# A hybrid attention layer on one core: the last gate's SiLU as a quotient, the first gates' SiLU and the last query's stores moved up, one unit's maxima moved into the first attention blocks, and the late w_out splits on other engines

## The chip, the cores and the metric

The kernel runs on one core of a Trainium2 chip. Its time is the device time of one execution in microseconds; three executions of the kernel before took 723.15, 723.17 and 726.25 us, median 723.17. A core has TensorE (PE; its weight loads are listed as PEld), VectorE (DVE), ScalarE (ACT), GpSimd (POOL) and SyncE (SP, which only issues DMAs). Each engine runs its own instructions in order; between engines an instruction waits for semaphores.

## The reference, cut to what matters

One layer of a diffusion backbone: a modulated RMSNorm, one projection whose columns are queries, keys, values and gates of two groups of heads, attention for each group, a SiLU gate, one output projection.

```python
h = rmsnorm(xs, norm_gain[l]) * (1.0 + scale) + shift
q_a, k_a, v_a, g_a, q_b, k_b, v_b, g_b = project(h, w_in[l], ...)
...
o_a = global_attn_latent(q_a, k_a, v_a, cache_k_a[:, l], cache_v_a[:, l])
o_b = window_attn_latent(q_b, k_b, v_b, cache_k_b[:, l], cache_v_b[:, l], sink_b[l])
xs = xs + gate * merge_out(o_a, g_a, o_b, g_b, w_out[l])

def merge_out(o_a, g_a, o_b, g_b, w_out):
    return jnp.concatenate([o_a * jax.nn.silu(g_a), o_b * jax.nn.silu(g_b)], axis=-1) @ w_out
```

There are 1024 latent tokens and 128 context tokens (nine tiles of 128), a model width of 1024, and in each group 8 query heads of 64 over 2 key heads. All is float32; the softmax subtracts the row's maximum.

## The kernel before, in words

Every float32 product is made of two rounded parts: a matrix is split into a high part (a cast) and a low part (the rest after a subtraction), and high·high, high·low and low·high are added in PSUM. So nearly each tensor that feeds TensorE costs a cast on one engine and a subtraction on another.

The stages, in order of time:

1. **Modulation, norm and the first gates** (0 to about 72 us). Tokens are normed and transposed on TensorE into `px`; ScalarE turns `px` into `hf` (L401; three buffers with the tag `hf`), VectorE casts it (L406), GpSimd subtracts (L407). While they arrive, the gates of group A for the first 768 tokens accumulate in six PSUM banks (`big`, four of 512 tokens, and `small`, two). After the loop over `j` the gates' SiLU, `put_gates` (L289), reads each bank, and a DMA stores the result to `g_dram`. Its tiles `sg` take the buffers of the tag `hf` too. Then the products for the last 384 tokens follow (`pg`, L262), first into the bank that `big[0]` held.
2. **Queries** (to about 214 us). For each group `m` and tile `t` a projection `pq`, and behind it four steps that `later(n, ...)` puts some half blocks behind: `squares`, `scale`, `rotated`, `turned`. `turned` transposes (`ptq`, L622), casts the high part `qo0q` (L625) and stores it; `low` subtracts the low part `qo1q` on VectorE (L630), and its store follows another half block later. Both stores are DMAs on ScalarE's own queue (L635), in line with its other work. There are two buffers for `qo1q`.
3. **Keys and values** (to about 270 us). Projections `pk`, then `sqk` (L763) and the value cast `v_hi` (L752) on ScalarE, a chain of some ten VectorE instructions, a doubled copy `k2k` on ScalarE (L721), a transpose `ptk` on TensorE (L727), and the low parts `klp`, `kla`, `klb` on VectorE (L745). The first three `pk` are computed during the last queries, and their chains run after them. `v_hi` and its neighbours lie where the query stage's buffers lay, and so wait for the last query stores.
4. **Gates of group B** (`gates(W_GB, 1, ...)`, to 314.9 us): twelve pieces of 24 matmuls, each closed by a SiLU. Between the matmuls stand the items of `beside[2]`: for the units in `EARLY` (units 0 and 2) the row maxima of the global scores, `pmx` (L858), with VectorE's `mx` reductions (L859), and `finish`, which makes the negated maxima `m_nat`. A transpose `ptm` (L877) and a VectorE multiplication by `diag` (L878) turn these into the last four rows of `qb`. VectorE also splits ten of the sixteen blocks of `w_out` there (`split_wo`, L1014 a cast, L1015 the subtraction, which is on GpSimd for odd blocks).
5. **Attention** (to the end). 36 units: for a tile `t`, a key head `g` and a group `m`; units 0, 2, 4, ... are global ones with nine key blocks, units 1, 3, 5, ... windowed ones with three or four. A slot is one block. In a global slot TensorE makes the scores `st` (L1097 with `qt`, L1098 with `qb`, which holds the maxima), ScalarE the exponential `pe` (L1100) and the cast `ph` (L1104), GpSimd the low part `pl` (L1108), and three slots later TensorE the values `pv` (L1118 to L1121). Between these stand items for later units: the maxima of the unit two further on at `MX_AT`, and the windowed scores `sn` (L915, L916) of the next unit at `NAT_AT`, with VectorE's mask and row minimum (L919) and ScalarE's `pen` (L905). `pmx`, `ptm`, `sn` share the two PSUM banks with the tag A; `st` has the two of tag B. The last five blocks of `w_out` are loaded and split here, at the slots of `WO_LATE`.

The order on an engine is that of the Python emission; `in_order` fixes it. `later(n, f)` runs `f` after `n` ticks, and a tick is half a projection block in stages 1 to 4 and one slot in stage 5. The exponential's table is loaded on ScalarE by an instruction of its own (L1046) behind the last SiLU.

Of the kernel before, what the change touches and what calls it, by code (L numbers as in the profile page):

```python
# [9 lines left out]
F32 = mybir.dt.float32  # L10
# [3 lines left out]
ALU = mybir.AluOpType  # L14
# [4 lines left out]
P = 128  # L19
# [16 lines left out]
PL_DVE = (4,)  # L36
LAG = 3
LEAD = 4
EARLY = (0, 2)
LOADED = 4  # L40


NAT_AT = (0, 1, 2, 3)
NAT_FIRST = (0, 1, 2, 3)
MX_AT = (-4, -3, -2, -2, -1, 4, 5, 5, 7, 7, 8, 8)
MX_FIRST = (0, 1, 2, 2, 3, 4, 4, 5, 6, 6, 7, 8)
PH_DVE = 0
MX_END = 10
SPLIT_LAG = 2
# [23 lines left out]
ROWS_AT = (1, 1, 4, 6)  # L73
KV_ORDER = [0] + list(range(1, NT))
GATE_AT = (3, 7)
QUERY_LAST = (0, 1, 2, 4)
CACHE_AT = 8
VC_AT = 6
ONES_AT = 14
# [28 lines left out]
def hybrid_step(ctx, tc, x_prompt, x_sample, cache_k_a, cache_v_a, cache_k_b, cache_v_b,  # L108
# [17 lines left out]
    def later(n, f):  # L126

        agenda.setdefault(now[0] + n, []).append(f)
# [156 lines left out]
    def put_gates(pg, m, ch, ts):  # L285

        n = ts.stop - ts.start
        sg = sg_tile[-1](f"sg{m}_{ch}_{ts.start}")[:, 0:n]
        nc.scalar.activation(sg, pg, AF.Silu)  # L289
        r0 = 512 * m + P * ch  # L290
        (nc.scalar, nc.sync)[m].dma_start(g_dram[r0 : r0 + P, ts], sg)

    def put_pair(pg, ch):

        sg = sg_tile[-1](f"sgp{ch}")
        nc.scalar.activation(sg, pg, AF.Silu)
        nc.scalar.dma_start(g_dram[P * ch : P * ch + 2 * P, 512:768].rearrange("(c p) n -> p c n", p=P),
                            sg.rearrange("p (c n) -> p c n", c=2))

    def gates(w, m, nxt, thirds):  # L300

        pieces = [(ch, slice(a, b)) for a, b in thirds for ch in range(4)]
        for ch, ts in pieces:
            pg = bank_mm(f"pg{m}_{ch}_{ts.start}")[:, 0 : ts.stop - ts.start]
            block(pg, lambda k: gate_products(pg, w, ch, ts, k), nxt, nxt and (ch, ts) == pieces[-1])
            later(1, lambda pg=pg, ch=ch, ts=ts: put_gates(pg, m, ch, ts))
            yield


# [1 line left out]
    with tc.tile_pool(name="st", bufs=2, side="right") as st:  # L311
# [129 lines left out]
        for j in range(KT + 2):  # L441
# [30 lines left out]
                first_gates(1, j - 1, 1)  # L472
            if j == 1:
                transposed(0, 5, 2, 0)
            if big_on:
                first_gates(2, j - 1)
            if j < KT:
# [24 lines left out]
        assert not second  # L502


        sg_tile.append(lambda n: st.tile([P, 512], F32, tag="hf", name=n, bufs=3))
        put_gates(big[0], 0, 0, slice(0, 512))
        for ch in range(1, 4):
            later(ch, lambda ch=ch: put_gates(big[ch], 0, ch, slice(0, 512)))
        for i in range(2):
            later(4 + i, lambda i=i: put_pair(small[i], 2 * i))  # L510
        for _ in gates(W_GA, 0, W_QA, THIRDS[2:]):
            pass
        tick()
# [37 lines left out]
    with tc.tile_pool(name="qt", bufs=2, side="right") as qt:  # L551
# [34 lines left out]
        def query(pq, m, t, tabs, n=1):  # L586

            nm = f"q{m}_{t}"
            pqv = pq.rearrange("p (h d) -> p h d", d=HD)
            v = {}  # L590

            def squares():
                sq = qt.tile([P, 8, HD], F32, tag="sq", name=f"sq{nm}")
# [25 lines left out]
            def turned():  # L619
                ptq = bank_tr(f"pt{nm}")  # L620
                for h in range(4):
                    nc.tensor.transpose(ptq[:, P * h : P * h + P], v["qf"][:, h].rearrange("p g d -> p (g d)"),  # L622
                                        ident_r.bitcast(F32))
                qo = [qt.tile([P, 512], F32R, tag=f"qo{i}", name=f"qo{i}{nm}") for i in range(2)]
                nc.scalar.copy(qo[0], ptq)  # L625
                put(qo[0], 0)
                later(1, lambda: low(ptq, qo))

            def low(ptq, qo):
                nc.vector.tensor_tensor(qo[1], ptq, qo[0], op=ALU.subtract)  # L630
                later(1, lambda: put(qo[1], 1))

            def put(part, i):
                for g in range(2):
# [372 lines left out]
            wo_big[a] = h_slot(a // 2, 2, 4 * (a % 2), f"wo_big{a}")  # L1007
        return wo_big[a][:, 512 * o : 512 * o + 512]

    def split_wo(i):  # L1010
        raw = wo_raw.pop(i)
        hi, lo = (wo_place(j, i) for j in range(2))
        wo_parts[i] = hi, lo
        nc.vector.tensor_copy(hi, raw)  # L1014
        (nc.gpsimd if i % 2 else nc.vector).tensor_tensor(lo, raw, hi, op=ALU.subtract)  # L1015


    mask = qp.tile([P, 512], BF16, name="mask", bufs=1)
# [15 lines left out]
        load_wo(i)  # L1034
    for i, at, *then in WO_STEPS:
        later(at, lambda i=i, then=then: wo_step(i, *then))
    for n, _ in enumerate(gb):
        if n == 4:
            for i in (7, 8, 9):
                load_wo(i)  # L1040
    for f in beside[2]:
        f()
    tick()
    p1.close()

    nc.scalar.add_instruction(mybir.InstLoadActFuncSet(  # L1046
        name=nc.get_next_instruction_name(), engine=mybir.EngineType.Activation, act_func_set_id=6))

    qp2.append(ctx.enter_context(tc.tile_pool(name="qp2", bufs=1, side="right")))
    w3 = ctx.enter_context(tc.tile_pool(name="w3", bufs=4, side="right"))  # L1050
# [188 lines left out]
    for s in range(len(slots) + LAG + PROMPT_END[3]):  # L1239
        tick()  # L1240
        if s < len(slots):
            live.append((slots[s], slots[s] and scores(slots[s][0], slots[s][1], slots[s][3])))
        for n, at in WO_LATE.items():
            if s == at:
                load_wo(n, w2)
                later(3, lambda n=n: split_wo(n))
        for f in due.get(s, ()):
            f()
        rate = OUTRATE if s < len(slots) and slots[s] else PADRATE
        credit = min(credit + rate, 6.0) if outq else 0.0  # L1250
        while outq and credit >= 1.0:
            outq.pop(0)()
            credit -= 1.0
        if s >= LAG and live:
            slot, parts = live.pop(0)
            if slot:
                values(*slot, *parts)
# [65 lines left out]
```

## Time and profile before

| what | value |
|---|---|
| three executions | 723.15, 723.17, 726.25 us |
| span of the profiled execution, first to last instruction | 721.3 us |
| mean granted TensorE clock | 0.993 |
| instructions | 10622 |
| DMA over the span | 78.56 MB, 109 GB/s |

The profile gives a span, and no device time of its own for that execution. The median of the three executions is 1.9 us above the span. Idle time in the profile's rows stands in square brackets, with the instruction that ended it. In the views of waits the columns are: who waited, for whom, us in total, times, longest.

### The profile page before, as it was taken

Reading aid. Unit: us, or ns where it says so; the run is one execution under the profiler, and the core shown is the slowest. Engines: PE = TensorE matmul, PEld = TensorE weight load, DVE = VectorE, ACT = ScalarE, POOL = GpSimd, SP = SyncE. Lnnn points to the kernel's source line nnn. Section 1 sums busy time; section 2 is a strip of 40 time slices with the busy share of each in tenths; the row PEclk is TensorE's granted clock in tenths of the full one; section 3 lists DMA queues with packets and bytes.
Section 4 is the critical chain, followed back from the end, with each engine's and each line's share of the span. In section 5 each row is a group of like instructions: output and inputs, shape, how many; then the busy total and the mean of one; then the engine's idle time right before and its main releaser. Section 6 shows DMA issues by size and latency. Waiting matters only on the chain. (4 is left out here: it accounts for less than half of the span.)

```text
span 721.3 us, 10622 instructions
## 1 busy us (share of the span) xinstructions
PE 698.3 (97%) x3524; PEld 559.7 (78%) x3524; DVE 457.6 (63%) x1007; ACT 411.7 (57%) x829; POOL 335.3 (46%) x355
## 2 busy tenths in 40 slices
PE   5999999999999999999999999999999999999997
PEld 2678988877777788977788888888888888887865
DVE  3466147875675872745866677577666775775653
ACT  5355411411232451158778877877787778877770
POOL 3456013332322340236666555655575557555751
PEclk9999999999999999999999999999999999999999
DMA  8961373348435115440321222121212221212323
GB/s 344 346 219 59 121 278 86 79 94 276 121 85 142 45 60 171 139 143 23 103 67 45 73 67 88 44 81 52 87 54 59 66 87 45 81 53 87 103 65 119
DMA packets 53159, 78.56 MB, mean 109 GB/s; under 512 B 6569, under 2 KB 25449, under 8 KB 52081
## 3 DMA queue, kind: packets, MB, share of 16 engines
q1 hardware_dynamic: 44928, 65.96, 28.1%
q10 hardware_dynamic: 8176, 11.94, 6.3%
q8 instruction: 28, 0.46, 0.3%
q14 instruction: 27, 0.21, 0.1%
HBM read 58.69 MB, written 19.18 MB: 108 GB/s over the span
## 5 line engine op out<-in xcount | busy, mean ns | idle before, releaser
L1108 POOL TENSOR_TENSOR pl<-pe,ph 128x512 fp32r<-128x512 f32 x130 | 167.6, 1292 | 144.7 <-DVE nm L919 67.5
L859 DVE TENSOR_REDUCE mx<-pmx 128x1 f32<-128x384 f32 x192 | 101.4, 552 | 59.5 <-PE pmx L858 58.1
L1100 ACT ACTIVATE pe<-st 128x512 f32<-128x512 f32 x146 | 86.8, 594 | 28.0 <-PE st L1098 27.1
L1104 ACT CAST ph<-pe 128x512 fp32r<-128x512 f32 x146 | 90.6, 621 | 4.8
L1118 PE MATMUL pv<-ph,v_hi 128*128 128x512 f32 x208 | 83.2, 400 | 2.2 <-DVE spare L1142 2.2
L1121 PE MATMUL pv<-pl,v_hi 128*128 128x512 f32 x208 | 82.6, 397 | 0.0
L173 POOL TENSOR_TENSOR rs_q<-ms_q,mhalf 128x8 f32<-128x8 f32 x18 | 34.8, 1931 | 82.1 <-DVE ms_q L171 82.1
L1189 PE MATMUL po<-wo,ogh 128*128 128x512 f32 x216 | 72.5, 394 | 0.2 <-DVE yt L1196 0.2
L919 DVE CUSTOM_DVE_ANT_0 sn<-sn,mask,nsink 128x512 f32<-128x512 f32 (+1 forms) x64 | 46.3, 724 | 38.3 <-PE sn L916 36.5
L858 PE MATMUL pmx<-kha,qt 128*128 128x384 f32 x192 | 61.0, 363 | 0.4 <-ACT pen L905 0.2
L1097 PE MATMUL st<-qt,kha 128*128 128x512 f32 x144 | 58.3, 405 | 1.5 <-ACT pe L1100 0.8
L1098 PE MATMUL st<-qb,kla 68*128 68x512 f32 x144 | 57.6, 400 | 1.1 <-DVE qb L878 1.1
L1120 PE MATMUL pv<-ph,v_lo 128*64 128x512 f32 x146 | 57.9, 396 | 0.0
L1121 PEld LDWEIGHTS pv<-pl,v_hi 128*128 128x128 f32 x208 | 39.4, 189 | 16.7 <-issue 0.2
L905 ACT ACTIVATE pen<-sn,nm 128x512 f32<-128x512 f32 (+2 forms) x72 | 45.0, 626 | 6.5 <-DVE nm L919 3.1
L1093 ACT CAST ph<-st 128x512 fp32r<-128x512 f32 x62 | 36.4, 587 | 19.9 <-PE st L1092 18.7
L1118 PEld LDWEIGHTS pv<-ph,v_hi 128*128 128x128 f32 x208 | 39.4, 189 | 10.5 <-ACT ogh L1154 2.4
L1189 PEld LDWEIGHTS po<-wo,ogh 128*128 128x128 f32 x216 | 40.0, 188 | 6.8 <-DVE yt L1196 0.6
L1094 DVE TENSOR_TENSOR pl<-st,ph 128x512 fp32r<-128x512 f32 x62 | 42.5, 686 | 2.3 <-ACT ph L1093 1.5
L1189 PE MATMUL po<-wo,ogl 128*128 128x512 f32 x108 | 42.6, 394 | 0.0
L594 ACT ACTIVATE sqq<-pq 128x512 f32<-128x512 f32 x18 | 10.8, 599 | 53.3 <-DMA qd<-qo0q 14.4
L858 PEld LDWEIGHTS pmx<-kha,qt 128*128 128x128 f32 x192 | 35.5, 190 | 6.2 <-DVE mx L859 1.4
(216 smaller groups left out, 1700.2 us busy)
## 6 DMA issues: line engine op xcount, KB each, us to landing
qt<-qd SPq DMA_DIRECT2D x36, 256.0 KB, 3.1
wm<-in_w_mod_ss_dram SPq DMA_DIRECT2D x8, 1024.0 KB, 5.1
qd<-qo0q ACTq DMA_DIRECT2D x36, 128.0 KB, 2.4
qd<-qo1q ACTq DMA_DIRECT2D x36, 128.0 KB, 2.4
sgl<-gd SPq DMA_DIRECT2D x36, 128.0 KB, 2.1
out_dram<-yt SPq DMA_DIRECT2D x17, 256.0 KB, 2.1
xn<-in_x_sample_dram SPq DMA_DIRECT2D x8, 512.0 KB, 7.0
wg<-in_w_mod_g_dram SPq DMA_DIRECT2D x4, 1024.0 KB, 7.9
```

The lines of the kernel that those rows point to most:

```text
L858: nc.tensor.matmul(pm[:, 0:384], lhs, kha[:, g, 3 * b : 3 * b + 3, :], start=True, stop=True)
L859: nc.vector.tensor_reduce(mx[:, h, b : b + 1], pm[:, 0:384], axis=AX.X, op=ALU.max)
L919: nc.vector.tensor_tensor_reduce(s, s, mask[:, m0 : m0 + n], -1.0, nsink[:, 4 * g + h : 4 * g + h + 1], op0=ALU.add, op1=ALU.min, accum_ou ...
L1097: nc.tensor.matmul(s, kh, qtile[i], start=True, stop=False)
L1098: nc.tensor.matmul(s, kl, qbtile[i], start=False, stop=True)
L1100: nc.scalar.activation(pe, s, AF.Exp)
L1104: nc.scalar.copy(ph, pe)
L1108: nc.gpsimd.tensor_tensor(pl, pe, ph, op=ALU.subtract)
L1118: nc.tensor.matmul(pv, two, ph, start=(b == 0), stop=False)
L1120: nc.tensor.matmul(pv[0:64, :], vl, ph, start=False, stop=False)
L1121: nc.tensor.matmul(pv, two, pl, start=False, stop=last)
L1189: nc.tensor.matmul(po[n], a, wo_parts[KT * n + k][lo], start=(k == KS[0] and p == 0), stop=(k == KS[-1] and p == 2))
```

## The change

- `EARLY` keeps unit 0 only. Unit 2's twelve `pmx` matmuls and `mx` reductions leave the gates' stage and stand in unit 0's slots 0 to 8 (`MX_FIRST`), with `finish` in slot 10 and `ptm` in slot 12. The four windowed score items of unit 1 move from slots 0 to 3 to slots 3 to 6 (`NAT_FIRST`). Unit 0's own maxima are spread over the same eight pieces as both were before.
- The last gate piece is not a SiLU on ScalarE any more but x / (1 + exp(-x)): an `Exp` on ScalarE, then an addition, a reciprocal and a multiplication on VectorE, each 128x384. The exponential's table is loaded half a piece earlier, ahead of that `Exp`.
- The first two `big` banks get their SiLU and store inside the loop at `j == KT`, ahead of the last seven `hf`.
- The last query (group B, tile 0) is turned half a block earlier, and its subtraction and both stores follow at once instead of by `later`.
- The late blocks of `w_out` are cast on ScalarE and subtracted on GpSimd, not on VectorE.

```diff
-EARLY = (0, 2)
+EARLY = (0,)
-NAT_FIRST = (0, 1, 2, 3)
+NAT_FIRST = (3, 4, 5, 6)
-MX_FIRST = (0, 1, 2, 2, 3, 4, 4, 5, 6, 6, 7, 8)
+MX_FIRST = (0, 0, 1, 1, 2, 2, 3, 4, 5, 6, 7, 8)
-QUERY_LAST = (0, 1, 2, 4)
+QUERY_LAST = (0, 1, 2, 3)
...
+    def put_quotient(pg, m, ch, ts):
+
+        n = ts.stop - ts.start
+        e = sg_tile[-1](f"e{m}_{ch}")[:, 0:n]
+        sg = sg_tile[-1](f"sg{m}_{ch}_{ts.start}")[:, 0:n]
+        nc.scalar.activation(e, pg, AF.Exp, scale=-1.0)
+        nc.vector.tensor_scalar(e, e, 1.0, None, op0=ALU.add)
+        nc.vector.reciprocal(e, e)
+        nc.vector.tensor_tensor(sg, pg, e, op=ALU.mult)
+        r0 = 512 * m + P * ch
+        nc.sync.dma_start(g_dram[r0 : r0 + P, ts], sg)
...
-            later(1, lambda pg=pg, ch=ch, ts=ts: put_gates(pg, m, ch, ts))
+            put = put_quotient if m == 1 and (ch, ts) == pieces[-1] else put_gates
+            later(1, lambda pg=pg, ch=ch, ts=ts, put=put: put(pg, m, ch, ts))
...
+            if j == KT:
+                sg_tile.append(lambda n: st.tile([P, 512], F32, tag="hf", name=n, bufs=3))
+                for ch in range(2):
+                    put_gates(big[ch], 0, ch, slice(0, 512))
...
-        sg_tile.append(lambda n: st.tile([P, 512], F32, tag="hf", name=n, bufs=3))
-        put_gates(big[0], 0, 0, slice(0, 512))
-        for ch in range(1, 4):
-            later(ch, lambda ch=ch: put_gates(big[ch], 0, ch, slice(0, 512)))
+        for ch in range(2, 4):
+            later(ch - 1, lambda ch=ch: put_gates(big[ch], 0, ch, slice(0, 512)))
         for i in range(2):
-            later(4 + i, lambda i=i: put_pair(small[i], 2 * i))
+            later(3 + i, lambda i=i: put_pair(small[i], 2 * i))
...
+            after = (lambda f: f()) if (m, t) == (1, 0) else (lambda f: later(1, f))
...
-                later(1, lambda: low(ptq, qo))
+                after(lambda: low(ptq, qo))
...
-                later(1, lambda: put(qo[1], 1))
+                after(lambda: put(qo[1], 1))
...
-    def split_wo(i):
+    def split_wo(i, late=False):
...
-        nc.vector.tensor_copy(hi, raw)
-        (nc.gpsimd if i % 2 else nc.vector).tensor_tensor(lo, raw, hi, op=ALU.subtract)
+        (nc.scalar.copy if late else nc.vector.tensor_copy)(hi, raw)
+        (nc.gpsimd if i % 2 or late else nc.vector).tensor_tensor(lo, raw, hi, op=ALU.subtract)
...
+    def load_exp():
+        nc.scalar.add_instruction(mybir.InstLoadActFuncSet(
+            name=nc.get_next_instruction_name(), engine=mybir.EngineType.Activation, act_func_set_id=6))
+
     for n, _ in enumerate(gb):
...
+        if n == 6:
+            later(2, load_exp)
...
-                later(3, lambda n=n: split_wo(n))
+                later(3, lambda n=n: split_wo(n, True))
```

How the change moves instructions, at three places. First ScalarE at the end of the queries of group B, before (`_7`, `_8`, `_0` are the tiles, `qo0q` high parts, `qo1q` low parts, `qd` the stores' target):

```order
L635 DMA qd_1_70<-qo1q_6_2172 64x512 x2
L625 CAST qo0q_8_2268<-ptq_8_2263 128x512
L635 DMA qd_1_74<-qo0q_8_2268 64x512 x2
L625 CAST qo0q_0_2278<-ptq_0_2273 128x512
L635 DMA qd_1_58<-qo0q_0_2278 64x512 x2
L635 DMA qd_1_72<-qo1q_7_2229 64x512 x2
L635 DMA qd_1_74<-qo1q_8_2269 64x512 x2
L635 DMA qd_1_58<-qo1q_0_2279 64x512 x2
L763 ACTIVATE sqk_2334<-pk_2165 128x256
```

and the same place now:

```order
L651 DMA qd_1_70<-qo1q_6_2172 64x512 x2
L641 CAST qo0q_0_2254<-ptq_0_2249 128x512
L651 DMA qd_1_58<-qo0q_0_2254 64x512 x2
L651 DMA qd_1_58<-qo1q_0_2255 64x512 x2
L641 CAST qo0q_8_2281<-ptq_8_2276 128x512
L651 DMA qd_1_74<-qo0q_8_2281 64x512 x2
L651 DMA qd_1_72<-qo1q_7_2229 64x512 x2
L651 DMA qd_1_74<-qo1q_8_2282 64x512 x2
L779 ACTIVATE sqk_2334<-pk_2165 128x256
```

Tile 0's cast and all its stores have gone ahead of tile 8's; the last store in the queue is now that of tile 8's low part, and with two buffers that part takes the buffer of tile 0's, not of tile 7's.

Second VectorE at the end of the gates of group B, as it is now (`e1_3` and `sg1_3_768` belong to the last gate piece, `qb0` to unit 0, `mx2` and `pmx2` to unit 2):

```order
L885 TENSOR_REDUCE m40_3314<-mx0_3017 128x4
L888 TENSOR_SCALAR m_nat0_108<-m40_3314 128x4
L299 TENSOR_SCALAR e1_3_3323<-e1_3_3323 128x384
L300 RECIPROCAL e1_3_3323<-e1_3_3323 128x384
L301 TENSOR_TENSOR sg1_3_768_3324<-pg1_3_768_3282,e1_3_3323 128x384
L894 TENSOR_TENSOR qb0_3312<-ptm0_3353,diag_110 4x512
L875 TENSOR_REDUCE mx2_3365<-pmx2_0_0_3366 128x1
L875 TENSOR_REDUCE mx2_3365<-pmx2_0_1_3369 128x1
```

Before, unit 0's `qb` had been made some pieces earlier, and unit 2's stood at this place with nothing of the gates ahead of it:

```order
L1015 TENSOR_TENSOR wo1_10_3344<-wraw10_3259,wo0_10_3343 128x512
L859 TENSOR_REDUCE mx2_3192<-pmx2_3_2_3350 128x1
L869 TENSOR_REDUCE m42_3361<-mx2_3192 128x4
L872 TENSOR_SCALAR m_nat1_109<-m42_3361 128x4
L878 TENSOR_TENSOR qb2_3359<-ptm2_3394,diag_110 4x512
L919 ISA sn1_0_3411,nm1_3407<-sn1_0_3411,mask_2978,nsink_105 128x384
```

Third TensorE in the first slots of unit 0, as it is now (before, each pair of `st` was followed by a pair of `sn`):

```order
L893 MATMUL ptm0_3353<-ident_r_99,m_nat0_108 4x128
L1116 MATMUL st0_0_3356<-qt0_2981,kha_2319 128x512
L1117 MATMUL st0_0_3356<-qb0_3312,kla_2320 128x512
L874 MATMUL pmx2_0_0_3366<-kha_2319,qt2_2985 128x384
L874 MATMUL pmx2_0_1_3369<-kha_2319,qt2_2985 128x384
L1116 MATMUL st0_1_3372<-qt0_2981,kha_2319 128x512
L1117 MATMUL st0_1_3372<-qb0_3312,kla_2320 128x512
L874 MATMUL pmx2_0_2_3381<-kha_2319,qt2_2985 128x384
L874 MATMUL pmx2_1_0_3384<-kha_2319,qt2_2985 128x384
```

The second matmul of the first scores reads `qb0`, whose last writer on VectorE stands behind the three instructions of the quotient.

More of the change, by code (lines that the diff above doesn't have):

```diff
@@ L1044, in hybrid_step @@
     p1.close()
-    nc.scalar.add_instruction(mybir.InstLoadActFuncSet(
-        name=nc.get_next_instruction_name(), engine=mybir.EngineType.Activation, act_func_set_id=6))
     qp2.append(ctx.enter_context(tc.tile_pool(name="qp2", bufs=1, side="right")))
```

## The prediction

> **What bounds the kernel now.** I read the page first, then the view of waits for TensorE alone, then the timeline around each of its waits. The first table of the page (engine, busy us, share of the span, instructions) says which engine to follow:
>
> ```profile
> PE 698.3 (97%) x3524; PEld 559.7 (78%) x3524; DVE 457.6 (63%) x1007; ACT 411.7 (57%) x829; POOL 335.3 (46%) x355
> ```
>
> TensorE is busy for 97%, so an edit pays only if it removes matmuls or one of the few holes between them. The holes behind the start-up are these, of which the change aims at five:
>
> ```profile
> PE ptk L727 <- DVE klp L745: 1.4, 1, 1.4
> PE ptk L727 <- ACT k2k L721: 1.2, 1, 1.2
> ...
> PE pg L262 <- ACT sg L289: 0.9, 1, 0.9
> PE st L1097 <- ACT pe L1100: 0.8, 1, 0.8
> ...
> PE st L1097 <- DVE pl L1094: 0.7, 1, 0.7
> PE sn L915 <- ACT pen L905: 0.5, 1, 0.5
> ```
>
> They sum to 5.5 us, 0.8% of the span. To these belongs a hole that no wait shows: a slower clock behind the last gate. In the windows below the columns are busy time of PE, PEld, DVE, ACT, POOL with instruction counts, then the granted clock:
>
> ```profile
> 319.00:320.00 1.00, 1.00 (x4) 0.40 (x2) 0.55 (x2) 0.97 (x3) 0.62 (x2) 0.66 0.86 265
> 320.00:321.00 1.00, 0.90 (x3) 0.61 (x3) 0.14 (x2) 0.97 (x4) 1.00 (x1) 0.50 0.96 289
> 322.00:323.00 1.00, 1.00 (x4) 0.81 (x3) 0.24 (x2) 0.97 (x3) 0.83 (x1) 0.64 0.78 266
> ```
>
> After 0.8 and 0.5 us of idling within three, the clock was halved for some 3 us, which costs up to 1.6 us more. So everything that this change can win lies near 7 us, and what it can lose is new holes of the same kind.
>
> **First gates' SiLU.** ScalarE and TensorE before:
>
> ```profile
> 68.50 2.37 ACT L401 ACTIVATE hf<-px,b_col,a_mod 128x128 f32<-128x128 f32 x5 [2.70 <-PE px L397]
> 71.89 0.60 ACT L289 ACTIVATE sg<-pg_f 128x512 f32<-128x512 f32 x1
> 72.53 0.44 PE L262 MATMUL pg<-h,whiga 128*128 128x384 f32 x1 [0.94 <-ACT sg L289]
> ```
>
> Two SiLUs of 0.60 us and two store issues (0.55 at most, half of the query's pair below) make at most 2.3 us, and ScalarE idles 2.70 us ahead of 68.50: they fit, and the wait of 0.94 goes. But the SiLU's tiles are two of the three `hf` buffers, and a store lands some 2 us after its issue (2.4 for the query's below), so the second `hf` waits for the first store and the next ones follow GpSimd with two buffers. I count the last `hf` and the last `px` transposes 0.6 us late (two transposes wait for a bank, 0.2 to 0.3 each). Net −0.35 us. Bounds: −0.94 with no delay, +0.5 if the stores land slowly. If the idle 2.70 were not there, the two SiLUs would cost their 2.3 us in front of the `hf`.
>
> **Last query's stores.** The rows around them, and the page's row of the low parts' stores with the median us from issue to landing:
>
> ```profile
> 210.70 0.39 PE L250 MATMUL pk<-whikv,h 128*128 128x512 f32 x1
> 211.35 0.68 DVE L614 TENSOR_TENSOR qfq<-qnq,gain 128x512 f32<-128x512 f32 x1
> 213.65 1.04 PE L622 MATMUL ptq<-ident_r,qfq 128*128 128x128 f32 x8
> 216.79 1.10 ACTq L635 DMA_DIRECT2D qd<-qo0q  x2
> 221.22 0.69 DVE L630 TENSOR_TENSOR qo1q<-ptq,qo0q 128x512 fp32r<-128x512 f32 x1 [5.62 <-DMA qd<-qo1q]
> 223.09 0.39 ACT L763 ACTIVATE sqk<-pk 128x256 f32<-128x256 f32 x1 [6.32 <-DMA ksin<-in_k_sin_dram]
> 225.19 0.37 ACT L752 CAST v_hi<-pk 128x256 fp32r<-128x256 f32 x1 [1.72 <-DMA qd<-qo1q]
> 229.47 0.66 PE L727 MATMUL ptk<-ident_r,k2k 128*128 128x128 f32 x4 [1.17 <-ACT k2k L721]
> 237.53 0.63 PE L727 MATMUL ptk<-ident_r,k2k 128*128 128x128 f32 x4 [1.44 <-DVE klp L745]
> ```
>
> ```profile
> qd<-qo1q ACTq DMA_DIRECT2D x36, 128.0 KB, 2.4
> ```
>
> The last subtraction (221.22) waits for a landing that frees its buffer, the stores queue behind it on ScalarE, `sqk` starts when the queue is empty, `v_hi` when the stores have landed, and the chain of keys from there is late twice on TensorE. Now tile 0's transposes stand half a block earlier, where TensorE arrives at 210.93; its operand is ready at 211.35 + 0.68 = 212.03. That is a new hole of about 1.2 us, and `ptq_8` behind it finds its bank free to within 0.1: the next projection starts 1.3 us late. ScalarE then casts tile 0 at 212.9 to 213.5, issues four stores (1.1 per pair) until 215.7, casts tile 8 at 216.0, and issues three pairs until 219.9; tile 8's low part needs tile 0's buffer, whose stores land at about 217.5, in time. So `sqk` starts at 220.0, 3.1 us sooner than 223.09. TensorE comes 1.3 us later to both `ptk`, the chain 3.1 us sooner: both holes (1.17 and 1.44) close. Net 1.3 − 2.6 = −1.3 us. Bounds: −2.6 if the operand were in time, +0.5 if the chain is not sooner at all (the old holes then swallow the new one).
>
> **End of the gates, unit 0.** The rows:
>
> ```profile
> 299.96 0.34 PE L858 MATMUL pmx<-kha,qt 128*128 128x384 f32 x1
> 300.14 0.33 PE L262 MATMUL pg<-h,whigb 128*128 128x384 f32 x1
> ...
> 315.10 0.40 PE L1098 MATMUL st<-qb,kla 68*128 68x512 f32 x1
> ...
> 324.94 0.39 PE L1097 MATMUL st<-qt,kha 128*128 128x512 f32 x1
> ...
> 326.09 0.40 PE L1097 MATMUL st<-qt,kha 128*128 128x512 f32 x1
> ...
> 328.61 0.60 PE L1092 MATMUL st<-ident_r,pen 128*128 128x128 f32 x4
> ```
>
> ```profile
> 315.01 0.49 ACT L289 ACTIVATE sg<-pg 128x384 f32<-128x384 f32 x1 [4.21 <-PE ptm L877]
> 315.52 1.28 ACT L1046 ACT_TABLE_LOAD   x1
> 316.81 0.60 ACT L1100 ACTIVATE pe<-st 128x512 f32<-128x512 f32 x1
> ```
>
> A `pmx` takes 0.18 us of TensorE, a 512 wide matmul 0.23 (five in 1.15). (1) Twelve `pmx` and one `ptm` leave the gates' stage, where TensorE has no wait: −2.2 us. (2) The table load leaves the path: `pe` could start 1.3 us sooner. (3) It can't, since the first score's second matmul needs `qb0`, which VectorE makes behind the quotient. VectorE's prices, from groups by form and a single line's view:
>
> ```profile
> L859 DVE TENSOR_REDUCE mx<-pmx 128x1 f32<-128x384 f32 x192 | 101.4, 552 | 59.5 <-PE pmx L858 58.1
> L878 DVE TENSOR_TENSOR qb<-ptm,diag 4x512 fp32r<-4x512 f32 x18 | 12.3, 682 | 7.9 <-PE ptm L877 7.8
> L954 DVE RECIPROCAL inv<-sum 128x4 f32<-128x4 f32 x18 | 3.0, 168 | 1.1 <-POOL sum L951 1.1
> L171 DVE TENSOR_SCALAR ms_k<-ssk 128x4 f32<-128x4 f32 x9 | 1.5, 170 | 0.3
> L376 DVE TENSOR_SCALAR xn<-xn,rsx x9: 753/753/1791, 10.1 to 51.7; 128x1024 f32<-128x1024 f32 x9
> ```
>
> `Exp` ends at 315.50 as the SiLU did. The addition is 0.38 (753 ns for 1024 columns, less a fixed 0.15, by 384/1024), the multiplication 0.55 like `mx`, `qb` 0.68. A reciprocal of 384 columns isn't in the trace; one of 4 columns takes 168 ns, an ordinary instruction of 4 columns 170, so no extra per element shows, and I take 0.56. With hand-overs `qb0` is ready at 317.8 instead of TensorE's 315.10: +2.75 us, all of it idle TensorE.
>
> (4) From there to unit 1's first transposes the trace took 328.61 − 315.10 = 13.5 us. Now TensorE has to do 0.23, eight pairs of `st` (3.7), thirteen `pmx` (2.3), four pairs of `sn` (1.4) and six triples of values (4.2): 11.8 us. ScalarE's load in between is what it was (nine `pe` and `ph`, four `pen`). To the 11.8 come waits of `pmx` and `sn` for the two banks, each held for 0.34 + 0.55 us with two per slot at first: between 0 and 1.9 us, I take 1.2. And the clock: 2.6 us of idling in one piece is more than the 1.3 that halved it before, so I take it as halved again for 3.2 us, 1.6 us of which some lies beside those waits: 1.3. Sum 14.3, that is +0.8. The stage: −2.2 + 2.75 + 0.8 = +1.35 us; bounds −1.0 (no bank waits, full clock) and +2.5.
>
> The Trainium skill's page "TensorE: Matmul & The Clock Gate", section "Part 1: The HAM clock gate", has the clock fall only after at least one idle window of about 3.4 us. By that the 2.6 us here would leave it at full speed and the stage would cost 0.05 instead of 1.35. The rows above do not agree: 1.3 us of idling in pieces was enough.
>
> **Late w_out.** Three casts of blocks 11, 14, 15 and two of 12, 13 move to ScalarE, two of the subtractions with them to GpSimd. The one that mattered:
>
> ```profile
> 332.24 0.69 DVE L1015 TENSOR_TENSOR wo_big<-wraw,wo_big 128x512 fp32r<-128x512 f32 x1
> 333.68 0.47 PE L1097 MATMUL st<-qt,kha 128*128 128x512 f32 x1 [0.67 <-DVE pl L1094]
> 354.52 0.51 PE L1098 MATMUL st<-qb,kla 68*128 68x512 f32 x1 [0.63 <-DVE qb L878]
> ```
>
> The subtraction delayed `pl` and TensorE waited 0.67 us at unit 2's start. That goes, but unit 2's maxima now end where unit 4's did, so its `qb` is late as theirs was, 0.63 us: zero. ScalarE's added casts (about 0.6 each, a 128x512 pass like the SiLU's) lie in its idle time beside the windowed slots; without that cover the pace of the first exponentials behind them would carry them, at most 1.2 us per unit.
>
> **Sum.** −0.35 − 1.3 + 1.35 + 0 = −0.3 us on a span of 721.3. What lies outside the span (1.9 us to the median) is not touched, so 723.17 becomes 722.9.
>
> **Rivals.** *The reciprocal works several steps per element* (slower than before): eight would add 384 x 7 x 1.04 ns = 2.8 us to `qb0`'s wait (1.04 ns per column from 552 ns for 384, less 0.15), giving 725.7; slower than before from about two steps (0.4 us) on. For it: the trace has no long one. Against it: at 4 columns it would already show 29 ns. The skill's page "VectorE: DVE Perf Modes", section "First, the fixed hardware budget", says that the reciprocal's divide runs with a repeat count of 8, which read as eight steps an element gives that time; the 168 ns speak against it.
>
> *The clock stays full*: −1.3, so 721.6. For it: the idling is in one piece and might fall across two measuring windows. Against it: the rows above.
>
> *The key chain is not freed*, because `v_hi` waits for the landing of all stores and the last one is still late: then −1.3 becomes 0, and the time 724.2. Against it: the order has four stores fewer behind the last landing.
>
> **Chances.** The forecast 0.45, the reciprocal 0.15, the full clock 0.2, the chain 0.12, mixtures 0.08. 0.5% (3.6 us, about what a measurement of this kernel can tell from no change) lies at 719.6 and 726.8. Below that only the full clock with all lower bounds comes: 0.06. Above it the reciprocal with a second slow clock or the chain's failure: 0.07. Within: 0.87. The range 720.4 to 726.0 holds the three rivals and leaves out the ends of the bounds.
>
> **What would show it.** In the profile after: the wait on `sg` at 72.5 gone; a new wait of about 1.2 us of `ptq` for `qfq`, and both waits of `ptk` gone; a wait of about 2.6 us of the first `st` (on `qb`) behind the gates; windows at half clock behind it; the reciprocal's own row near 0.56 us. It is wrong if the first `st` waits under 1.5 us, if `sqk` starts no sooner, or if a stage beyond unit 4 changes its pace.

## The result: 726.0 us, 2.85 us slower, and the profile after

The changed kernel takes 725.99 us (median of 18 runs, 724.38 to 727.07), the kernel before 723.14 us in the same session (18 runs, 721.69 to 726.25). The ratio is 1.0036, 95% interval 1.0028 to 1.0045. The forecast was 722.9 us, a gain of 0.3 us; a loss of 2.85 us came. 725.99 lies just inside the range that the prediction gave (720.4 to 726.0), but the forecast had the sign wrong. The profiled execution has a span of 724.6 us (721.3 before).

The first table of the page after says the same of TensorE as before: busy for 97%, it is what bounds.

```profile
PE 699.3 (97%) x3524; PEld 560.4 (77%) x3524; DVE 455.9 (63%) x1003; ACT 414.9 (57%) x834; POOL 338.2 (47%) x357
```

The view of waits for TensorE (who waited, for whom, us in total, times, longest) has changed in the rows that the prediction spoke of. Both `ptk` rows and the row on `sg` are gone, and a new one leads:

```profile
PE st L1117 <- DVE qb L894: 6.1, 4, 4.6
...
PE ptq L638 <- DVE qfq L630: 1.1, 1, 1.1
...
PE px L410 <- ACT hf L414: 0.5, 1, 0.5
```

One wait of 4.6 us stands where about 2.6 were forecast. VectorE's timeline at that place (start, duration, instruction, idle time before it) shows what it waits for:

```profile
312.00 0.36 DVE L299 TENSOR_SCALAR e<-e 128x384 f32<-128x384 f32 x1 [2.25 <-ACT e L298]
312.40 2.55 DVE L300 RECIPROCAL e<-e 128x384 f32<-128x384 f32 x1
314.99 0.56 DVE L301 TENSOR_TENSOR sg<-pg,e 128x384 f32<-128x384 f32 x1
315.58 0.68 DVE L894 TENSOR_TENSOR qb<-ptm,diag 4x512 fp32r<-4x512 f32 x1
```

The reciprocal takes 2.55 us; the prediction had 0.56. The addition (0.36 for 0.38), the multiplication (0.56 for 0.55) and `qb` (0.68) are as forecast. On TensorE:

```profile
311.23 0.23 PE L893 MATMUL ptm<-ident_r,m_nat 128*4 128x128 f32 x1
311.29 0.45 PE L1116 MATMUL st<-qt,kha 128*128 128x512 f32 x1
316.31 0.80 PE L1117 MATMUL st<-qb,kla 68*128 68x512 f32 x1 [4.57 <-DVE qb L894]
```

And the windows behind it (columns as in the prediction):

```profile
315.00:316.00 1.00, 0.00 (x0) 0.00 (x0) 0.97 (x2) 0.00 (x0) 0.00 (x0) 0.54 0.00 0
316.00:321.00 5.00, 4.69 (x13) 3.71 (x13) 2.85 (x7) 3.27 (x6) 2.31 (x2) 0.50 0.76 216
321.00:322.00 1.00, 1.00 (x5) 0.90 (x4) 0.48 (x2) 0.69 (x2) 0.79 (x2) 0.55 1.02 360
```

TensorE is busy again from 316.31 on (4.69 of the five us from 316), but at half the clock until about 321.9, for twice as long as in the profile before.

Where the time went is read best from five marks in TensorE's timeline: the first matmul of the first gates' last piece (`pg` at 72.53 before), the last `ptm` ahead of unit 0, the first `st<-qb` of unit 0, the first transposes of unit 1 and those of unit 3. Units are counted from 0, as in the code; in some expectations below "unit 3's maxima" are what the code calls unit 2's. The table has the time from each mark to the next, in us, one profiled execution of each kernel; the labels are those of the experiments.

| kernel | `pg` at | to `ptm` | to `st<-qb` | to unit 1 | to unit 3 | to the end of TensorE |
|---|---|---|---|---|---|---|
| before | 72.53 | 242.23 | 0.34 | 13.51 | 19.90 | 368.06 |
| after | 72.96 | 238.27 | 5.08 | 15.01 | 20.06 | 368.15 |
| u_silu | 72.46 | 238.52 | 1.00 | 13.88 | 20.07 | 367.71 |
| silu_wo | 71.43 | 238.31 | 1.00 | 13.89 | 21.27 | 367.67 |
| silu_max | 71.89 | 240.46 | 0.34 | 13.05 | 20.33 | 368.06 |
| swap | 72.92 | 238.64 | 1.00 | 18.14 | 20.07 | 367.84 |
| short_recip | 71.66 | 238.45 | 3.28 | 14.31 | 20.07 | 367.78 |
| u_max | 71.37 | 240.57 | 0.34 | 16.32 | 20.10 | 368.05 |
| lnexp | 73.20 | 239.65 | 1.00 | 13.97 | 20.07 | 368.17 |
| only_max | 72.32 | 239.85 | 1.00 | 13.91 | 21.97 | 367.77 |
| only_query | 72.51 | 240.68 | 0.33 | 13.05 | 20.23 | 368.21 |

Of the kernel after, 3.96 us are won ahead of `ptm`, 4.74 are lost from there to `st<-qb`, 1.50 from there to unit 1, 0.25 behind, and 0.43 at the start. The last is within what executions differ by anyway: the mark lies between 71.4 and 73.2 in these kernels, which hardly differ before it. The way to `ptm` differs by 1 us between executions too: a second profile of u_silu's kernel (u_silu_2) has 239.54 there, and 1.00, 13.90, 20.08 and 367.62 behind, so the gains ahead of `ptm` named below are those of single executions.

### The profile page after: what moved, and what is told of

It reads as the page before. It is cut to its first block, busy times and chain, and to the rows that moved or that the text cites. A ratio compares the mean times of both kernels' runs of the same rounds, so it can differ in the third digit from the quotient of the medians.

```text
span 724.6 us, 10639 instructions
## 1 busy us (share of the span) xinstructions
PE 699.3 (97%) x3524; PEld 560.4 (77%) x3524; DVE 455.9 (63%) x1003; ACT 414.9 (57%) x834; POOL 338.2 (47%) x357
```

## The experiments

Two theories stood at first. **A**: the whole loss is the reciprocal, which stands on VectorE ahead of unit 0's `qb`; what else was changed gains. **B**: unit 2's maxima in the first slots cost, and the reciprocal only fills a hole that would be there without it. Each kernel was timed beside the kernel before on the same chip; ratios, with their 95% intervals, are to that one (723.2 to 723.4 us); they differ by up to 0.1% from the quotients of the two medians.

**u_silu: the quotient alone undone.**

```diff
-            put = put_quotient if m == 1 and (ch, ts) == pieces[-1] else put_gates
+            put = put_gates
...
-        if n == 6:
-            later(2, load_exp)
...
     p1.close()
+    load_exp()
```

> The changed kernel with the quotient alone undone: the last gate's SiLU is one ScalarE instruction again and the Exp table is loaded after it. Everything else of the change stays, unit 3's maxima in the first blocks too. Theory A (the 2.55 us reciprocal stands on VectorE ahead of unit 0's qb, opens the 4.57 us wait on TensorE and with it the 6.5 us of half clock, and that is the whole loss): st<-qb starts about 0.4 us after ptm as before, half clock about 3 us, 719.6 to 721.6 us. Theory B (unit 3's maxima in the first blocks are what costs, by their matmuls and bank waits at half clock, and the reciprocal only fills a hole that would be there anyway): 724 us or more.

720.62 us (ratio 0.9951, 0.9931 to 0.9970). Theory A's range held, B's did not. Two of A's signs came out otherwise: `st<-qb` starts 1.00 us behind `ptm`, not 0.4, and the clock does not fall at all. A second set of runs gave nearly the same:

> The same kernel as u_silu again (the quotient undone, all else of the change kept), since that had six runs only. If its 720.6 us was the kernel and not the chip or the hour: 720.0 to 721.3 us, 2 to 3 us below the kernel before.

720.36 us (0.9966, 0.9956 to 0.9976). So by the medians the quotient costs 5.4 to 5.6 us against the SiLU and table load that it replaced, and the other four parts are worth 2.8 us together. In the table, between after and u_silu, 4.08 us of the quotient's cost lie ahead of `st<-qb` and 1.13 between there and unit 1. ScalarE with the SiLU back, from its timeline:

```profile
311.23 0.49 ACT L289 ACTIVATE sg<-pg 128x384 f32<-128x384 f32 x1 [3.85 <-PE ptm L893]
311.74 1.28 ACT L1054 ACT_TABLE_LOAD   x1
313.03 0.60 ACT L1118 ACTIVATE pe<-st 128x512 f32<-128x512 f32 x1
```

The first `pe` starts at 313.03, 2.05 us behind `ptm`; with the quotient it starts at 317.14, 5.91 us behind:

```profile
317.14 0.60 ACT L1119 ACTIVATE pe<-st 128x512 f32<-128x512 f32 x1 [5.17 <-PE st L1117]
```

The table load that the quotient was to hide takes 1.28 us; the reciprocal alone takes 2.55. In the windows the clock stays full:

```profile
311.00:314.00 3.00, 2.47 (x10) 1.42 (x9) 1.93 (x4) 2.71 (x4) 0.00 (x0) 1.00 0.30 106
314.00:317.00 3.00, 2.99 (x14) 2.05 (x14) 2.67 (x7) 2.94 (x6) 2.59 (x3) 1.00 0.92 232
317.00:320.00 3.00, 2.57 (x13) 1.79 (x11) 1.95 (x5) 2.94 (x8) 2.45 (x2) 1.00 0.84 285
```

**short_recip: the reciprocal over 96 of 384 columns.**

```diff
-        nc.vector.reciprocal(e, e)
+        nc.vector.reciprocal(e[:, 0:96], e[:, 0:96])
```

> The changed kernel with the reciprocal over the first 96 of the 384 columns; the other columns of the last gate are multiplied by 1 + exp(-x) and are not the reference's. Only the length of the reciprocal differs. Theory A: it takes 0.7 to 0.8 us if its price goes by columns; the wait at st<-qb falls by 1.8 us to 2.8 us, the half clock gets shorter too, 723.0 to 724.3 us. Theory B: 725.5 us or more. If the wait falls but the time does not, the wait was not on the path.

723.84 us (0.9995, 0.9984 to 1.0006), 2.1 us below the kernel after, inside A's range and outside B's. VectorE's and TensorE's rows of this kernel's timeline:

```profile
311.28 0.75 DVE L300 RECIPROCAL e<-e 128x96 f32<-128x96 f32 x1
...
313.39 0.54 PE L1117 MATMUL st<-qb,kla 68*128 68x512 f32 x1 [2.77 <-DVE qb L894]
```

1.80 us less of reciprocal is 1.80 us less of waiting (4.57 to 2.77), and 0.70 us less from there to unit 1 (15.01 to 14.31 in the table); the half clock lasts 3.4 us here, not 6.8.

**swap: `qb` ahead of the quotient's vector part.** The three instructions of VectorE are put off until behind `qb`; the order of the other instructions around them, on VectorE, ScalarE and TensorE, stays as it was.

```diff
         nc.scalar.activation(e, pg, AF.Exp, scale=-1.0)
-        nc.vector.tensor_scalar(e, e, 1.0, None, op0=ALU.add)
...
+        def rest():
+            nc.vector.tensor_scalar(e, e, 1.0, None, op0=ALU.add)
...
+        later(2, rest)
...
-    tick()
+    for _ in range(3):
+        tick()
     p1.close()
```

> The changed kernel with unit 0's qb ahead of the quotient's three VectorE instructions; same instructions on every engine. The reciprocal now stands ahead of unit 3's first maxima in place of qb. Theory A: the 4.57 us wait at st<-qb falls below 0.8 us; the third pmx matmul of unit 3 waits some 2 us for a bank in its place; 722.5 to 724.5 us. Theory B (the position ahead of qb does not matter, VectorE is simply short by 3.5 us in the first blocks): 725.5 to 726.5 us.

724.88 us (1.0013, 0.9998 to 1.0027): 1.1 us below the kernel after, and between the ranges of A (up to 724.5) and B (from 725.5). The wait moved, to the third `pmx`, whose bank VectorE had not read:

```profile
312.56 0.50 PE L1122 MATMUL st<-qb,kla 68*128 68x512 f32 x1 [0.49 <-DVE qb L898]
316.60 1.15 PE L878 MATMUL pmx<-kha,qt 128*128 128x384 f32 x2 [2.72 <-DVE mx L879]
```

The clock fell again, and for as long (windows of the same kernel):

```profile
315.00:316.00 1.00, 0.00 (x0) 0.00 (x0) 0.96 (x3) 0.49 (x1) 1.00 (x2) 0.86 0.00 0
...
322.00:323.00 1.00, 1.00 (x5) 0.76 (x5) 0.00 (x0) 0.17 (x2) 0.80 (x1) 0.73 1.08 319
```

In the table 4.08 us are won at `st<-qb` and 3.13 lost from there to unit 1, so the place ahead of `qb` is not the main point.

**u_max: the maxima back in the gates' stage, the quotient kept.**

```diff
-EARLY = (0,)
+EARLY = (0, 2)
-NAT_FIRST = (3, 4, 5, 6)
+NAT_FIRST = (0, 1, 2, 3)
-MX_FIRST = (0, 0, 1, 1, 2, 2, 3, 4, 5, 6, 7, 8)
+MX_FIRST = (0, 1, 2, 2, 3, 4, 4, 5, 6, 6, 7, 8)
```

> The changed kernel with the maxima alone put back into the gates' stage; the quotient stays. Unit 0's qb is then made pieces earlier and unit 2's stands behind the quotient. Theory A (the reciprocal costs by standing ahead of the first score's qb): no wait of st<-qb at the first blocks, unit 1's sn matmuls wait 0 to 1.5 us for a bank instead, clock full or half for a short time, 721.0 to 723.0 us. Rival (3.5 us of VectorE there cost wherever they stand): 724.5 us or more.

725.15 us (1.0029, 1.0016 to 1.0042), in the rival's range and only 0.8 us below the kernel after. Unit 0's `qb` is there in time, and now unit 1's `sn` waits:

```profile
317.02 0.69 PE L931 MATMUL sn<-khb,qt 128*128 128x384 f32 x1 [3.52 <-DVE qb L894]
```

Against the same kernel with the SiLU (silu_max, below) the quotient costs 1.9 us in the medians and 3.1 in the profiled executions (645.38 and 642.24, sums of the table's rows); that is less than the 5.5 us it costs with the maxima in the first slots, but a loss still. Theory A was too narrow. What counts is that VectorE is shut for 3.5 us, from the addition's start to the multiplication's end, at a moment when TensorE needs it within a slot for something: for `qb`, for a maximum's bank, or for `sn`'s.

**lnexp: the quotient without VectorE's reciprocal.** ScalarE makes 1 / (1 + exp(-x)) as exp(-ln(1 + exp(-x))); VectorE only multiplies, behind `qb`.

```diff
         nc.scalar.activation(e, pg, AF.Exp, scale=-1.0)
-        nc.vector.tensor_scalar(e, e, 1.0, None, op0=ALU.add)
-        nc.vector.reciprocal(e, e)
+        nc.scalar.activation(e, e, AF.Ln, bias=1.0)
+        nc.scalar.activation(e, e, AF.Exp, scale=-1.0)
```

> The changed kernel with unit 0's qb ahead and the quotient made by ScalarE: after exp(-x) a Ln of that plus 1 and an Exp of its negative, VectorE only multiplies. All three are of the table that the attention needs, so no load stands between. Theory A (what counts is that neither VectorE nor ScalarE holds back the first score for long): pe comes about 1.8 us behind ptm, as with the SiLU and its table load, 719.6 to 721.4 us. Rival (two more ScalarE passes ahead of the first pe open the hole again): 722 us or more.

722.50 us (0.9981, 0.9966 to 0.9997). The median lies in the rival's range (722 or more) and outside A's 719.6 to 721.4. Yet the hole that the rival named is not in the profile: `pe` starts at 314.61, 1.76 us behind `ptm`, and the table has 1.00, 13.97 and 20.07 for it where u_silu has 1.00, 13.88 and 20.07. In its profiled execution most of the difference lies ahead of `ptm`, a part of it in the last query: a subtraction waited 1.68 us for a store's landing, where u_silu's waited 0.30 (VectorE's rows of lnexp, then of u_silu):

```profile
216.44 0.69 DVE L650 TENSOR_TENSOR qo1q<-ptq,qo0q 128x512 fp32r<-128x512 f32 x1 [1.68 <-DMA qd<-qo1q]
```

```profile
214.16 0.69 DVE L646 TENSOR_TENSOR qo1q<-ptq,qo0q 128x512 fp32r<-128x512 f32 x1 [0.30 <-DMA qd<-qo1q]
```

Both kernels have the same instructions at that place, in the same order, and u_silu's own kernel waited 1.71 us there in its second profile (u_silu_2), an execution that took 720.43 us. So this wait comes in some executions and not in others, and it does not explain the median. What makes lnexp's median 1.9 to 2.1 us longer than u_silu's stays open.

**only_max: the kernel before with the maxima alone moved** (the same three lines as in u_max, the other way round).

> The kernel before with unit 3's maxima alone moved from the gates' stage to the first blocks. Theory A: ptm comes about 2.2 us sooner and the first blocks give back 0 to 2 us of it: 721.0 to 723.2 us. Theory B: 724 us or more.

723.66 us (0.9999, 0.9987 to 1.0012), above A's range and under B's 724: nothing won or lost. The table says why. 2.38 us are won ahead of `ptm` and 1.06 given back up to unit 1, as A had it; but from unit 1 to unit 3 another 2.07 go (21.97 for 19.90). VectorE's timeline there:

```profile
330.21 0.41 DVE L1014 CAST wo_big<-wraw 128x512 fp32r<-128x512 f32 x1
330.66 0.69 DVE L1015 TENSOR_TENSOR wo_big<-wraw,wo_big 128x512 fp32r<-128x512 f32 x1
331.27 0.68 DVE L1094 TENSOR_TENSOR pl<-st,ph 128x512 fp32r<-128x512 f32 x1
331.87 0.55 DVE L859 TENSOR_REDUCE mx<-pmx 128x1 f32<-128x384 f32 x1
332.34 0.17 DVE L954 RECIPROCAL inv<-sum 128x4 f32<-128x4 f32 x1
332.42 0.40 DVE L1014 CAST wo_big<-wraw 128x512 fp32r<-128x512 f32 x1
332.85 0.68 DVE L878 TENSOR_TENSOR qb<-ptm,diag 4x512 fp32r<-4x512 f32 x1
```

Three passes of late `w_out`, 1.5 us, stand on VectorE ahead of unit 2's `qb`, which is made here now, and TensorE waits 0.70 us for `pl` and 1.01 us for `qb`:

```profile
332.11 0.47 PE L1097 MATMUL st<-qt,kha 128*128 128x512 f32 x1 [0.70 <-DVE pl L1094]
...
333.59 0.50 PE L1098 MATMUL st<-qb,kla 68*128 68x512 f32 x1 [1.01 <-DVE qb L878]
```

Behind these waits the clock is halved, from 334.5 to 337.9. That is the case that the last part of the change is for.

**silu_wo: u_silu with the late w_out splits back on VectorE.**

```diff
-        (nc.scalar.copy if late else nc.vector.tensor_copy)(hi, raw)
-        (nc.gpsimd if i % 2 or late else nc.vector).tensor_tensor(lo, raw, hi, op=ALU.subtract)
+        nc.vector.tensor_copy(hi, raw)
+        (nc.gpsimd if i % 2 else nc.vector).tensor_tensor(lo, raw, hi, op=ALU.subtract)
```

> The changed kernel with the quotient undone (as in u_silu) and also the late w_out splits put back on VectorE. Units are counted from 0 here, as in the code. Theory A (with unit 2's maxima in unit 0's slots VectorE is full around unit 2's start, so the late splits there cost what only_max lost: waits of 0.7 and 1.0 us on TensorE and half clock behind them): 1.4 to 2.4 us above u_silu, 722.0 to 723.0 us. Rival, the prediction's term (the late splits are worth nothing): 720.2 to 721.2 us.

722.59 us (0.9992, 0.9979 to 1.0005), 2.0 to 2.2 us above u_silu, as A said. The waits of TensorE between 325 and 335 us, of this kernel and then of u_silu:

```profile
PE st L1116 <- DVE qb L894: 1.0, 1, 1.0
PE st L1115 <- DVE pl L1112: 0.7, 1, 0.7
```

```profile
PE st L1116 <- DVE qb L894: 0.5, 1, 0.5
PE sn L931 <- ACT spare L987: 0.3, 1, 0.3
```

In the profiled executions that is 1.20 us (21.27 for 20.07). The waits are those of only_max, but the half clock that A named behind them did not come: the profiled execution, the fastest of the twelve (720.79 us), is at full clock here. The rest of the medians' distance is not placed.

**only_wo: the kernel before with these splits alone moved.** (The same two lines the other way round.)

> The kernel before with the late w_out splits alone taken off VectorE. The prediction's term: nothing. Theory A (the splits cost only where VectorE is full, which in the kernel before is one wait of 0.67 us): 0 to 0.7 us below before. Rival (they cost 1.2 us or more wherever the maxima stand, as silu_wo showed): 1.2 us or more below before.

723.30 us (1.0001, 0.9990 to 1.0011). Alone the move shows no gain, as predicted (the interval is 0.7 us below to 0.8 above); with the maxima, the last query and the first gates moved too it is worth about 2 us. So it pays where the maxima are moved; no run has these two parts without the other two.

**silu_max: u_silu with the maxima back** (the three lines of u_max).

> The changed kernel with the quotient undone and unit 2's maxima (counted from 0) back in the gates' stage: first gates, last query and late w_out are left. Theory A (the maxima are worth 2.2 us of TensorE less about 1.0 that the first blocks take longer, once the late splits are off VectorE): 1.0 to 1.6 us above u_silu, 721.6 to 722.4 us. Rival (the maxima are worth nothing, as only_max shows): 720.2 to 721.0 us.

723.23 us (0.9998, 0.9987 to 1.0009), 2.6 to 2.9 us above u_silu and above both ranges; A had 1.0 to 1.6 more. The profiled executions differ by 0.1 to 1.1 us from `pg` to the end (642.24 here, 641.18 and 642.14 in the two profiles of u_silu's kernel, sums of the table's rows), and the one here is the fastest of its twelve (721.44 us). The medians' distance goes along with the clock: the median of the runs' mean granted clocks is 0.993 here and 0.997 and 0.998 in the two runs of u_silu. Where it fell in the slower executions no trace shows, so the maxima's worth in the whole change is known by the medians alone.

**only_query: the kernel before with the last query's stores alone moved up.**

```diff
-QUERY_LAST = (0, 1, 2, 4)
+QUERY_LAST = (0, 1, 2, 3)
...
+            after = (lambda f: f()) if (m, t) == (1, 0) else (lambda f: later(1, f))
...
-                later(1, lambda: low(ptq, qo))
+                after(lambda: low(ptq, qo))
...
-                later(1, lambda: put(qo[1], 1))
+                after(lambda: put(qo[1], 1))
```

> The kernel before with the last query's stores alone moved up. The prediction's term: ptq waits 1.1 us, both ptk waits go, 1.3 to 1.8 us below the kernel before. Rival (the key chain is not freed, or TensorE loses it again behind): within 0.5 us of before.

722.70 us (0.9996, 0.9981 to 1.0011). In the profile the step does what was said: the wait on `qfq` is 1.09, `sqk` comes at 220.87 instead of 223.09, and the way to `ptm` is 1.55 us shorter.

```profile
212.06 0.63 PE L623 MATMUL ptq<-ident_r,qfq 128*128 128x128 f32 x4 [1.09 <-DVE qfq L615]
...
220.87 0.39 ACT L764 ACTIVATE sqk<-pk 128x256 f32<-128x256 f32 x1 [4.36 <-DMA qd<-qo1q]
```

In the medians only 0.5 us of it shows, less than the 1.3 to 1.8 expected; the interval holds anything from a gain of 1.4 to a loss of 0.8, so the runs decide neither way.

**only_first: the kernel before with the first gates' SiLU alone moved up.**

```diff
+            if j == KT:
+                sg_tile.append(lambda n: st.tile([P, 512], F32, tag="hf", name=n, bufs=3))
+                for ch in range(2):
+                    put_gates(big[ch], 0, ch, slice(0, 512))
...
-        put_gates(big[0], 0, 0, slice(0, 512))
-        for ch in range(1, 4):
-            later(ch, lambda ch=ch: put_gates(big[ch], 0, ch, slice(0, 512)))
+        for ch in range(2, 4):
+            later(ch - 1, lambda ch=ch: put_gates(big[ch], 0, ch, slice(0, 512)))
```

> The kernel before with the first gates' SiLU alone moved up. The prediction's term: 0.35 us below before, 0 to 0.9. Rival (the wait on sg goes and one on hf, of about 0.5 us, takes its place): within 0.4 us of before.

723.33 us (1.0000, 0.9991 to 1.0008): no gain, though the interval (0.7 us below to 0.6 above) still holds the forecast. The profile is clearer. The 0.94 us on `sg` is gone, and this stands in its place:

```profile
69.83 0.33 PE L397 MATMUL px<-ident,xn 128*128 128x128 f32 x1 [0.49 <-ACT hf L401]
```

ScalarE did not get both SiLUs into its idle time, since the first waited for a buffer that GpSimd was still reading:

```profile
67.17 0.60 ACT L289 ACTIVATE sg<-pg_f 128x512 f32<-128x512 f32 x1 [1.25 <-POOL h L407]
```

The last transposes of `px` start at 72.26, before at 70.94, with the first `pg_f` at 17.49 and 17.47. So 1.3 us are lost where 0.94 are won, and `pg` starts 0.2 us later than before (72.73 for 72.53).

## Why the prediction was wrong, point by point

**The reciprocal, the step that failed.** The prediction read 168 ns for a reciprocal of four columns beside 170 for an ordinary instruction, found "no extra per element", and took 0.56 us for 384. By the two longer sizes now measured the price is a fixed 0.15 us and 6.25 ns a column ((2553 − 752) / 288 from 384 and 96 columns, and 752 − 96 x 6.25 = 152). That is six times the 1.04 ns of an ordinary pass. At four columns the extra over an ordinary pass is 21 ns, less than the prediction's 29 for eight steps, and the row of 168 shows none of it: the line through the longer two gives 177 there. The rival with several steps per element is what happened, and its chance of 0.15 was too low. That its 725.7 us for eight steps lies so near the measured 725.99 is partly luck: at the measured six it gives 2.0 us more than the forecast, 724.9, and the rest came from the terms below. The Trainium skill's page "VectorE: DVE Perf Modes", section "First, the fixed hardware budget", gives the divide a repeat count of 8; read as steps per element that is nearer to the measured six than the one that was taken, though not equal to it.

**The wait on `qb`**: +2.75 forecast, +4.74 measured (0.34 to 5.08). The difference of 2.0 is the reciprocal's.

**The path from there to unit 1**: +0.8 forecast, +1.50 measured, and not by the parts named. Of the 1.2 us of waits for banks 0.2 came, while the half clock lasted 6.8 us and not 3.2. With the full clock the same path takes 13.88 us (u_silu), 13.97 (lnexp) and 13.91 (only_max) where the sum without the clock's term had 13.0; the half clock adds 1.1 to that, not 1.3. The 13.5 of the kernel before held a half clock too: with the same code there at full clock the path takes 13.04 (only_first) and 13.05 (only_query). So that half clock cost 0.5 us on this path, not "up to 1.6", and up to unit 3 only 0.1 of it is left (33.41 for 33.30 and 33.28 from `st<-qb` on).

**The maxima leaving the gates' stage**: −2.2 forecast, −2.38 measured (only_max). **The last query**: −1.3 forecast, −1.55 in the profile of only_query; both add up to the 3.96 of the kernel after. The hole of 1.1 us, the end of both `ptk` waits and the earlier `sqk` are as described; `sqk` came 2.0 us sooner, not 3.1.

**The first gates**: −0.35 forecast, no gain measured (only_first), with an interval that can't tell the two apart. In its profile the last `px` transposes come 1.3 us late, not 0.6, and the wait that the rows name is that of the first SiLU for a buffer of GpSimd's, 1.25 us. That the second `hf` waited for the first store, as the prediction had it, no row names.

**Late w_out**: nothing forecast, and from unit 1 to unit 3 the kernel after is 0.16 us slower than before. What the prediction did not see is that the zero is a balance: the maxima cost 1.2 us there at full clock if the splits stay (silu_wo) and 2.1 with a half clock behind (only_max), and the splits' move pays that back. The wait of unit 2's `qb` that was forecast at 0.63 came, 0.52 us.

**The rival that the clock stays full**: the row that the prediction held against it, a clock halved by waits of 0.8 and 0.5 us, decides nothing. The same waits (0.80 us, and 0.48 to 0.50) left the clock full in only_first, only_query and silu_max, and halved it again in only_wo. What the clock hangs on is worked out in the last section; by that a single wait of 4.57 us, or of the 2.6 forecast if most of it falls into one window, halves it. Without the quotient (u_silu) it stayed full in the profiled execution, and the kernel took 720.4 to 720.6, where this rival had 721.6.

## The version that beats both

u_silu, the change without the quotient, takes 720.6 and 720.4 us in two sessions, 2.8 us below the kernel before (ratios 0.9951 and 0.9966) and 5.4 to 5.6 below the kernel after. It is the fastest kernel that was run.

## What to carry to other kernels

A price read at a tiny size says next to nothing of the price per element: 168 ns for four columns allow anything up to 42 ns a column, and the true 6.25 can't be told from 1.04 there. When work is moved to an idle engine, look for who needs that engine within the next slot; a block of 3.5 us on a queue that is idle on average opened a hole of 2.7 to 4.6 us wherever it was put. And parts of a change should be tried both alone and taken away: the maxima and the late splits each showed no gain alone, and each costs about 2 us or more by the medians when it alone is taken out of u_silu.

## What was not expected of the hardware

The half clock comes in lengths of 3.4 us and 6.8 us. With a share x of a window at full clock its mean is 0.5 + 0.5x: before it fell at 319.32 (mean 0.66) and rose at 322.72 (0.64), 3.4 us; after, at 315.08 (0.54) and 321.90 (0.55), 6.8 us; in swap at 315.72 (0.86) and 322.54 (0.73), 6.8 us. The Trainium skill's page "TensorE: Matmul & The Clock Gate", section "Part 1: The HAM clock gate", has a free-running window of about 3.4 us and only two speeds; the lengths agree. It lets the clock fall after a window that is idle; here a window far from idle was enough.

The traces show where those windows lie. In each that has more than one change of the clock, the changes lie whole multiples of 3.413 us apart: before it also fell at 18.94, 300.38 us or 88.0 windows ahead of 319.32, and after at 18.12, 296.96 us or 87.0 windows ahead of 315.08. The offset is another in each execution. With it known, TensorE's busy time in the window ahead can be set beside what the clock did at its end:

| kernel | window from (us) | clock in it | TensorE busy, of 3.41 us | clock behind it |
|---|---|---|---|---|
| after | 311.67 | full | 0.07 | half |
| short_recip | 310.29 | full | 0.64 | half |
| swap | 312.31 | full | 1.32 | half |
| only_max | 331.11 | full | 1.70 | half |
| before | 315.91 | full | 2.12 | half |
| only_first | 315.52 | full | 2.20 | full |
| only_query | 316.02 | full | 2.43 | full |
| after | 315.08 | half | 2.18 | half |
| swap | 315.72 | half | 2.53 | half |
| before | 319.32 | half | 3.31 | full |
| short_recip | 313.70 | half | 3.41 | full |

In the 14 traces, from 25 us to 712, the clock fell behind every window with up to 1.70 us of busy time and behind none with 2.20 or more; between 1.95 and 2.13 it fell in two of five (three windows of the keys' stage kept it full). A halved clock stayed so behind windows of 2.18 to 2.63 us and rose behind those of 3.31 or more. So what counts is how much TensorE idles within one window, not how long one wait is: the same 0.8 and 0.5 us fell into one window in the kernel before and were cut by an edge in only_query. And waits of nearly the same length in short_recip and swap (2.77 and 2.72 us) gave 3.4 and 6.8 us at half clock, since swap's next window was busy for 2.53 us only.

The mean granted clock differs between executions of one kernel too. In 96 executions of the kernel before it lies between 0.990 and 1.000: 17 at 1.000 have a median of 722.08 us, 12 at 0.995 one of 723.27, 5 at 0.990 one of 726.05. At the same 0.995 the kernel after takes 725.16 us (5 runs), 1.9 us more. The rest of the 2.85 us goes along with a lower mean clock (median 0.993 after, 0.997 before), which the new hole itself brings: 6.8 us at half clock lower the mean over the span by 0.005.
